# Twenty transposes of the identity at the start, one sigmoid for all gates, one projection block moved ahead of the retention

## The chip, the cores and the metric

The kernel runs on one core of one Trainium2 chip. The metric is the device time of one execution in microseconds; less is better. All data are float32; the products run in pairs of rounded parts (see below).

## What is computed

Two transformer-like blocks are applied to x (1024 tokens of 1024 channels). The first block has a root-mean-square norm, one wide input projection `h @ w_in`, a retention branch, a sparse attention branch (NSA) whose three parts are weighted by sigmoid gates, a merge of the two branches by two more gates, and a gated convolution MLP. The second block has a condition-dependent norm, an RWKV and a state-space mixer, and a second MLP. The change lies in the first block alone:

```python
h = rmsnorm(x, norm_mix)
proj = h @ w_in
(rq, rk, rv, rg, nq, kcr, vcr, ksl, vsl, kwn, vwn, ngate, ga, gb) = split(proj)
y_a = retention(rq, rk, rv, rg, ret_gn_g) @ w_ret_o          # 4 heads, chunks of 128 tokens
y_b = nsa(nq, ..., ngate, ...) @ w_nsa_o                     # gt = sigmoid(ngate): 24 gates per token
merged = sigmoid(ga) * y_a + sigmoid(gb) * y_b
x = x + merged @ w_out
...
# retention, per head: inner product within a chunk, and a state R carried from chunk to chunk
o = (q k^T * dmask) v + (q * xi) R ;  R = decay * R + (k * zeta)^T v
out = silu(g) * groupnorm(o)
```

## The kernel before

Activations lie with channels on the partitions (`a`, eight tiles of 128 x 1024, each as a rounded part `hh` and a rest `hl`). A weight block of 128 columns is loaded by `wload` (L197) into one of two `wraw` buffers, rounded by ScalarE into `whi` (L199), and its rest is made by GpSimd into `wlo` (L202, four instructions); `wload2` (L212 to L216) does the same for a block of 256 columns into `w2hi` and `w2lo` of a pool of its own. `mm3` (L226) then makes 24 matmuls of 512 columns for each half of the tokens, and `mm3t` (L234) 24 for each tile of 128 tokens. `proj` takes its result banks from the pool `PM`, which has two; a bank is free again when its result has been copied out.

The order is made by a planner: each engine has its own list of instructions, in the order in which a simulated timeline found them ready, with the order of the program as priority. On the chip each engine, and each of the queues that issue DMAs (all of this kernel's on SP), works through its list strictly in order.

The stretches that the change touches, in the order of time:

- `first_norm` (L854 on) loads x in eight tiles. For each, ScalarE sums the squares (L867), DVE scales (L281, L869), and after four tiles TensorE turns them by `transpose` (L179), a product with the identity `ident`. ScalarE and DVE copy the result out as `hh` (L877) and `hl` (L878). The identity and the ones come by the first two DMAs.
- `values_gates` (L421 on) projects values and the 24 gates of each token: eight tiles, three times eight matmuls each (L234). The bank is read by ScalarE (L452, the copy L439, the sigmoid L440) and DVE (L453). `compress` (L456 on), which stands behind it in the program, uses a Gelu (L474).
- The attention follows, with 23 projection blocks (`gate_out`, L663 on, whose results go to `d_gab`) woven into it. 28 such blocks exist; the five left over are the function `rest`.
- `retention` runs four heads and then calls `rest()`. A head (`retention_head`, L671 on) projects its values with `wload2` and `mm3t`, then works through eight chunks that hang on one another by the state R, and writes `d_yr` (L748). Its pools lie in the memory that the attention gives back. Beside the heads a side job reads `w_ada` on DVE.
- `merge` loads `d_yr` back as `yrh`, `yrl` (L777, L778), makes the sixteen halves `w_nsa_o` x `yn`, each multiplied with a gate that is loaded from `d_gab` (L343), put through the sigmoid L784 and used in L802, and then the `w_ret_o` x `yr` halves. The gates have three buffers.

Of the kernel before, what the change touches and what calls it, by code (L numbers as in the profile page):

```python
# [9 lines left out]
F32 = mybir.dt.float32  # L10
F32R = mybir.dt.float32r
AF = mybir.ActivationFunctionType
# [72 lines left out]
    return c  # L85


LINE = 512
FIRST = 16512
TOP = 480  # L90
# [28 lines left out]
class Ctx:  # L119
# [26 lines left out]
    def fill(self, pool, at=0):  # L146

        n = -(at + pool.current_size() // 128) % LINE
        if n:
# [128 lines left out]
    def rsqrt(self, r, x, scale, eps):  # L278
# [3 lines left out]
        nc.scalar.activation(r, r, AF.Sqrt)  # L282
        nc.vector.reciprocal(r, r)

    def products(self):

        ins = self.nc.cur_bb.bb.instructions
        out = [i for i in ins[self.n_ins:] if i.engine == mybir.EngineType.PE]
        self.n_ins = len(ins)
        return out  # L290
# [102 lines left out]
class Nsa:  # L393
# [27 lines left out]
    def values_gates(self, tp):  # L421

        g, nc, w_in = self.g, self.g.nc, self.w_in
        w = [tp.tile([128, KT, 280], F32R, name=f"vw{x}") for x in "hl"]
        for c0, c, n in ((0, C_VS, 128), (128, C_VW, 128), (256, C_NG, 24)):
            raw = g.W.tile([128, KT, 128], F32, name="wraw", bufs=2)[:, :, :n]
            nc.sync.dma_start(raw, w_in[:, c:c + n].rearrange("(k p) n -> p k n", p=128))
            hi, lo = (z[:, :, c0:c0 + n] for z in w)
            nc.scalar.activation(hi, raw, AF.Copy)
            nc.gpsimd.tensor_sub(lo, raw, hi.bitcast(F32))  # L430
        self.new_values()
        for i in range(8):
            ps = g.PM.tile([128, 512], F32, name="mm")
            g.mm3t(ps[:, :280], w, self.a, slice(i * 128, (i + 1) * 128))
            v = ps[:, :256].rearrange("p (b g c) -> p b g c", b=2, g=2)
            self.split_values(self.vst[i // 4][:, i % 4], v[:, :, 0])
            if i % 4 == 0:
                v1 = g.st.tile([128, 512], F32, name="st").rearrange("p (i b c) -> p i b c", i=4, b=2)
            nc.scalar.copy(v1[:, i % 4], v[:, :, 1])  # L439
            nc.scalar.activation(self.gate[:, i], ps[:, 256:280], AF.Sigmoid)  # L440
            if i % 4 == 3:
                nc.sync.dma_start(self.v1(i // 4), v1.rearrange("p i b c -> p i (b c)"))

    def v1(self, t):
        return self.dv[t * 512:(t + 1) * 512].rearrange("(i p) c -> p i c", p=128)
# [216 lines left out]
def gate_out(g, a, w_in, c, dst, n):  # L662

    def ev(t, ps):
        o = g.st.tile([128, 512], F32, name="st")
        g.evac(t, o, ps)
        g.nc.sync.dma_start(dst[n * 128:(n + 1) * 128, t * 512:(t + 1) * 512], o)
    g.proj(w_in[:, c:c + 128], a, ev)
# [82 lines left out]
def retention(g, a, w_in, gn_g, D_, yp, side_job, rest, early):  # L751


    with ExitStack() as cx:
        P = {n: cx.enter_context(g.pool("r" + n)) for n in ("vp", "tp")}
        P.update({n: cx.enter_context(g.pool("r" + n, b, space=PSUM)) for n, b in (("p1", 2), ("p2", 2), ("p3", 1))})
        sp = cx.enter_context(g.pool("rsj"))
        P.update({n: g.const(n, P["tp"]) for n in ("zeta", "xi")})
        for h in range(4):
            retention_head(g, a, w_in, gn_g, D_["gab"], D_["yr"], h, P, early)  # L760
            if h == 0:
                yn = load_split(g, yp, D_["yn"], 4, "yn")
            if h == 1:
                r = side_job(sp)
        rest()
    return r, yn


def load_split(g, pool, src, nk, name):

    out = tuple([pool.tile([128, S], F32R, name=f"{name}{x}{k}") for k in range(nk)] for x in "hl")
    for t in range(2):
        get = g.stream(src, t, g.st)
        for k in range(nk):
            x = get(k)
            sl = slice(t * 512, (t + 1) * 512)
            g.nc.scalar.activation(out[0][k][:, sl], x, AF.Copy)  # L777
            g.nc.vector.tensor_sub(out[1][k][:, sl], x, out[0][k][:, sl].bitcast(F32))  # L778
    return out
# [64 lines left out]
def params1(g, I):  # L844
    par = g.params("a", [("norm_mix", col(I["norm_mix"][0])), ("norm_ffn", col(I["norm_ffn"][0])), ("norm_final", col(I["norm_final"])),
                         ("gn_g", col(I["ret_gn_g"][0])), ("b1_k", col(I["cmp_b1_k"][0])), ("b1_v", col(I["cmp_b1_v"][0])),
                         ("pos_k", I["cmp_pos_k"][0].rearrange("(l r) d -> l (r d)", r=2)),
                         ("pos_v", I["cmp_pos_v"][0].rearrange("(l r) d -> l (r d)", r=2))])
    par.update(g.params("b", [("conv_w", I["conv_w"][0].rearrange("i (r p) -> (i r) p", p=128)), ("conv_b", col(I["conv_b"][0]))]))
    return par  # L850


def first_norm(g, gain, a):

    nc = g.nc
    with g.pool("xl", 8) as lp, g.pool("xs", 2) as tp, g.pool("xlp", 4, space=PSUM) as pp:
        tiles = []
        for i in range(8):
            x = lp.tile([128, D], F32, name="xin")
            nc.sync.dma_start(x, g.I["x"][0][i * 128:(i + 1) * 128, :])  # L860
            tiles.append(x)
            if i == 3:
                gain = gain()
        for i, x in enumerate(tiles):
            ss = g.small((128, 1))
            sq = tp.tile([128, D], F32, name="xsq")
            nc.scalar.activation(sq, x, AF.Square, accum_out=ss)  # L867
            g.rsqrt(ss, ss, 1.0 / D, EPS)
            nc.vector.tensor_scalar(x, x, ss, None, op0=OP.mult)  # L869
            if i % 4 == 3:  # L870
                sl = slice((i - 3) * 128, (i + 1) * 128)
                for k in range(KT):
                    ps = pp.tile([128, 512], F32, name="xtp")
                    for j in range(4):
                        g.transpose(ps[:, j * 128:(j + 1) * 128], tiles[i - 3 + j][:, k * 128:(k + 1) * 128])
                    hi, lo = a[0][k][:, sl], a[1][k][:, sl]
                    nc.scalar.activation(hi, ps, AF.Copy, scale=gain[:, k:k + 1])  # L877
                    nc.vector.scalar_tensor_tensor(lo, ps, gain[:, k:k + 1], hi.bitcast(F32), op0=OP.mult, op1=OP.subtract)  # L878
# [3 lines left out]
CUT = (12, 11)  # L882
# [44 lines left out]
def nsa_phase(g, par, D_):  # L927


    I = g.I  # L930
    w_in, gab = I["w_in"][0], D_["gab"]
    hp = g.alloc("hp", side="right")
    a = tuple([hp.tile([128, S], F32R, name=f"h{x}{k}") for k in range(KT)] for x in "hl")
    g.st = g.alloc("st", 3)
    g.W = g.alloc("W")

    def gain():
        par.update(params1(g, I))
        return par["norm_mix"]
    first_norm(g, gain, a)  # L940
    cols = [C_RG + 128 * n for n in range(8)] + [C_GA + 128 * n for n in range(16)]
    fill = [(24 + 2 * h + e, c + 128 * h) for h in range(EARLY) for e, c in enumerate((C_RQ, C_RK))]
    fill += [(n, cols[n]) for n in [*range(8), *range(16, 24), *range(8, 16)]]
    with ExitStack() as cx:
        N = Nsa(g, a, w_in, par, D_["yn"], D_["nv"], cx)
        with g.pool("cp") as cp:
            N.cmp_proj(cp)
            N.group_proj(0)
            N.values_gates(cp)
            N.compress(cp)  # L950
        N.tp = cx.enter_context(g.pool("at", 2))
        for n, b in (("pct", 1), ("pth", 2), ("ptl", 2)):
            N.tp.tile([128, 512], F32R, name=n, bufs=b)
        for gr in range(2):
            if gr:
                N.group_proj(gr)
            N.select(gr)
            parts = N.attend(gr)
            for n, c in fill[gr * CUT[0]:CUT[0] + gr * CUT[1]]:
                gate_out(g, a, w_in, c, gab, n)  # L960
            beside_attention(g.tc, parts, g.products())
    return a, hp, lambda: [gate_out(g, a, w_in, c, gab, n) for n, c in fill[sum(CUT):]]


def block1(g, par, D_, side_job):

    I = g.I
    a, hp, rest = nsa_phase(g, par, D_)
    with g.pool("mgy") as yp:
        r, yn = retention(g, a, I["w_in"][0], par["gn_g"], D_, yp, side_job, rest, EARLY)  # L970
        hp.release()
        m = merge(g, D_, I, yn)
    g.WX = g.alloc("WX")
    return r, m
# [1048 lines left out]
```

## Time and profile before

| | us |
|---|---|
| median of 3 runs | 3440.11 |
| lowest and highest of the 3 | 3436.26, 3441.54 |
| the profiled execution, its time | 3434.05 |
| the profiled execution, first to last instruction (span) | 3432.3 |
| TensorE busy in the span | 3325.8 |

The profiled execution lies 6.06 us under the median of the runs, and 1.75 us of its own time lie outside its span. "PE" is TensorE, "DVE" VectorE, "ACT" ScalarE, "POOL" GpSimd, "SP" the queue that issues the DMAs. L with a number is a line of the kernel; a transpose has the helper's line L179 wherever it is called from. The mean granted TensorE clock of the span is 0.989 of full speed.

### The profile page before, as it was taken

What the parts mean: (1) busy time and instruction counts of PE and PEld (TensorE: products, weight loads), DVE (VectorE), ACT (ScalarE), POOL (GpSimd) and SP (SyncE); (2) the same over time, 40 slices, a digit from 0 to 9 for tenths busy, and PEclk for the clock granted to TensorE, in tenths of its full rate; (3) what the DMA queues carried; (4) which work ended last, traced back from release to release, by engine and by line L of the source; (5) the groups of instructions that cost most, each with busy time, mean ns of one, the idle gap of its engine ahead of it and who ended that gap; (6) DMA issues with size and microseconds to landing.
All of it is one profiled execution on the core that took longest, in us unless ns stands there. A gap on an engine that the chain in (4) does not pass through costs nothing. (4 is left out here: it accounts for less than half of the span.)

```text
span 3432.3 us, 51013 instructions
## 1 busy us (share of the span) xinstructions
PE 3325.8 (97%) x19080; PEld 2702.8 (79%) x19080; DVE 1593.4 (46%) x3313; ACT 1323.1 (39%) x2165; POOL 1699.6 (50%) x2221
## 2 busy tenths in 40 slices
PE   8999999999999999999999999999999999999998
PEld 6888888898788777888887777778777777688887
DVE  4356556555523674355564454653634343341112
ACT  5245446422334322344244344433443343342223
POOL 2343444321245656576776454355764343365554
PEclk9999999999999999999999999899999999999999
DMA  4211221455634434344533222144442122263332
GB/s 150 67 60 46 64 66 42 142 165 189 212 114 142 126 103 144 92 120 146 188 107 115 67 62 70 56 157 129 138 134 70 48 68 65 90 194 98 89 95 93
DMA packets 519826, 371.13 MB, mean 108 GB/s; under 512 B 31724, under 2 KB 455834, under 8 KB 518810
## 3 DMA queue, kind: packets, MB, share of 16 engines
q1 hardware_dynamic: 519578, 367.86, 34.8%
q8 instruction: 151, 2.47, 0.3%
q14 instruction: 97, 0.79, 0.1%
HBM read 313.44 MB, written 54.03 MB: 107 GB/s over the span
## 5 line engine op out<-in xcount | busy, mean ns | idle before, releaser
L202 POOL TENSOR_TENSOR wlo<-wraw,whi 128x256 fp32r<-128x256 f32 (+1 forms) x1552 | 1196.4, 801 | 1081.8 <-ACT whi L199 570.2
L199 ACT ACTIVATE whi<-wraw 128x1024 fp32r<-128x1024 f32 (+2 forms) x460 | 417.2, 909 | 792.6 <-PE mm L226 454.0
L226 PE MATMUL mm<-fh,whi 128*128 128x512 f32 x976 | 399.5, 411 | 3.2 <-ACT whi L199 2.5
L226 PE MATMUL mm<-fl,whi 128*128 128x512 f32 x976 | 390.4, 401 | 8.0 <-DVE fl L337 8.0
L226 PE MATMUL mm<-fh,wlo 128*128 128x512 f32 x976 | 269.3, 405 | 0.0
L226 PE MATMUL mm<-hh,whi 128*128 128x512 f32 x640 | 258.5, 404 | 3.7 <-DVE kc L255 2.8
L226 PE MATMUL mm<-hl,whi 128*128 128x512 f32 x640 | 259.0, 405 | 0.0
L226 PEld LDWEIGHTS mm<-fl,whi 128*128 128x128 f32 x976 | 184.9, 190 | 48.6 <-DVE fl L337 11.2
L226 PEld LDWEIGHTS mm<-fh,whi 128*128 128x128 f32 x976 | 184.7, 190 | 47.5 <-issue 4.7
L226 PE MATMUL b<-fh,whi 128*128 128x512 f32 x544 | 212.3, 390 | 0.4 <-DVE yo L255 0.4
L226 PE MATMUL b<-fl,whi 128*128 128x512 f32 x544 | 211.9, 390 | 0.0
L226 PEld LDWEIGHTS mm<-fh,wlo 128*128 128x128 f32 x976 | 179.2, 190 | 40.1 <-issue 3.3
L226 PE MATMUL mm<-ah,whi 128*128 128x512 f32 x429 | 177.0, 415 | 11.0 <-ACT ah L1621 8.4
L226 PE MATMUL mm<-hh,wlo 128*128 128x512 f32 x640 | 178.3, 400 | 0.0
L226 PE MATMUL mm<-al,whi 128*128 128x512 f32 x429 | 172.5, 403 | 0.2 <-DVE al L1622 0.2
L226 PE MATMUL b<-fh,wlo 128*128 128x512 f32 x544 | 139.1, 392 | 5.2 <-POOL wlo L202 5.2
L226 PEld LDWEIGHTS mm<-hh,whi 128*128 128x128 f32 x640 | 121.2, 189 | 25.8 <-issue 3.2
L226 PEld LDWEIGHTS mm<-hl,whi 128*128 128x128 f32 x640 | 121.2, 189 | 20.8
L226 PEld LDWEIGHTS mm<-hh,wlo 128*128 128x128 f32 x640 | 117.0, 188 | 21.8
L597 POOL TENSOR_SCALAR s<-s,ast 128x640 f32<-128x640 f32 (+7 forms) x128 | 88.1, 708 | 78.4 <-DVE ast L595 48.9
L226 PE MATMUL mm<-ah,wlo 128*128 128x512 f32 x429 | 126.0, 405 | 0.2 <-POOL wlo L202 0.2
L226 PEld LDWEIGHTS b<-fh,wlo 128*128 128x128 f32 x544 | 101.6, 188 | 29.1 <-POOL wlo L202 8.6
(600 smaller groups left out, 6976.8 us busy)
## 6 DMA issues: line engine op xcount, KB each, us to landing
wraw<-in_w_up SPq DMA_DIRECT2D x88, 512.0 KB
wraw<-in_w_in SPq DMA_DIRECT2D x84, 512.0 KB
ada_w<-in_w_ada SPq DMA_DIRECT2D x96, 256.0 KB
wraw<-in_ffn_w_gate SPq DMA_DIRECT2D x44, 512.0 KB
wraw<-in_ffn_w_up SPq DMA_DIRECT2D x44, 512.0 KB
wraw<-in_w_out SPq DMA_DIRECT2D x32, 512.0 KB
d_gab<-st SPq DMA_DIRECT2D x56, 256.0 KB
wraw<-in_w_down SPq DMA_DIRECT2D x48, 256.0 KB
```

Of the source, the lines that this page charges most:

```text
L199: nc.scalar.activation(hi[:, :kt], raw[:, :kt], AF.Copy)
L202: nc.gpsimd.tensor_sub(lo[:, sl], raw[:, sl], hi[:, sl].bitcast(F32))
L226: self.nc.tensor.matmul(ps, w[x][:, k], a[y][k][:, t * 512:(t + 1) * 512], start=i == 0, stop=i == 3 * kt - 1)
L597: nc.gpsimd.tensor_scalar(sb[r][:, :n], sb[r][:, :n], st[:, 2, r:r + 1], 1.0, op0=OP.mult, op1=OP.mult)
```

## The change

Three edits are made. `warm` is new: after the first four loads of x are issued, TensorE turns the identity twenty times into one bank, and DVE copies the last result over the identity itself, so that each later transpose depends on it. In `values_gates` the sigmoid of each of the eight tiles becomes a copy, and one sigmoid over all eight stands behind the loop. `rest` becomes a list of five functions; the first is called ahead of the four heads, the other four where all five were.

```diff
+WARM = 20
@@ class Ctx
+    def warm(self):
+        ps = self.PN.tile([128, 512], F32, name="pn")
+        for i in range(WARM):
+            self.transpose(ps[:, i % 4 * 128:(i % 4 + 1) * 128], self.ident)
+        self.nc.vector.tensor_copy(self.ident, ps[:, (WARM - 1) % 4 * 128:((WARM - 1) % 4 + 1) * 128])
@@ def values_gates
-            nc.scalar.activation(self.gate[:, i], ps[:, 256:280], AF.Sigmoid)
+            nc.scalar.copy(self.gate[:, i], ps[:, 256:280])
             if i % 4 == 3:
                 nc.sync.dma_start(self.v1(i // 4), v1.rearrange("p i b c -> p i (b c)"))
+        nc.scalar.activation(self.gate, self.gate, AF.Sigmoid)
@@ def retention
+        rest[0]()
         for h in range(4):
             retention_head(g, a, w_in, gn_g, D_["gab"], D_["yr"], h, P, early)
...
-        rest()
+        for x in rest[1:]:
+            x()
@@ def first_norm
             if i == 3:
+                g.warm()
                 gain = gain()
@@ def nsa_phase
-    return a, hp, lambda: [gate_out(g, a, w_in, c, gab, n) for n, c in fill[sum(CUT):]]
+    return a, hp, [lambda n=n, c=c: gate_out(g, a, w_in, c, gab, n) for n, c in fill[sum(CUT):]]
```

## Rows read from the trace of the kernel before

**Rows 1.** The page: busy us of each engine (share of the span), instructions.

```profile
PE 3325.8 (97%) x19080; PEld 2702.8 (79%) x19080; DVE 1593.4 (46%) x3313; ACT 1323.1 (39%) x2165; POOL 1699.6 (50%) x2221
```

**Rows 2.** The waits of TensorE: who waited for whom, us in all, times, longest.

```profile
PE mm L234 <- ACT w2hi L214: 3.3, 2, 2.3
PE mm L234 <- ACT gate L440: 3.1, 1, 3.1
...
PE mm L226 <- DVE kc L255: 2.8, 1, 2.8
...
PE mm L226 <- DVE yb L802: 2.5, 3, 1.5
```

**Rows 3.** The timeline, start: start us, us, engine, line, operation, count, [idle before <-releaser].

```profile
6.60 0.15 DVE L281 TENSOR_SCALAR sm<-sm 128x1 f32<-128x1 f32 x1 [6.60 <-ACT xsq L867]
...
9.12 1.12 PE L179 MATMUL xtp<-c_ident,xin 128*128 128x128 f32 x4 [9.12 <-DVE xin L869]
...
13.58 1.06 ACT L867 ACTIVATE xsq<-xin 128x1024 f32<-128x1024 f32 x1 [1.11 <-DMA xin<-in_x]
...
17.61 2.82 PE L179 MATMUL xtp<-c_ident,xin 128*128 128x128 f32 x12 [2.99 <-DVE hl L878]
...
22.34 0.48 PE L226 MATMUL mm<-hh,whi 128*128 128x512 f32 x1
...
29.71 0.60 PE L179 MATMUL xtp<-c_ident,xin 128*128 128x128 f32 x4
```

**Rows 4.** Windows: stretch, length, busy us of PE, PEld, DVE, ACT, POOL (instructions), PEclk, DMA, GB/s.

```profile
17.60:21.60 4.00, 3.82 (x17) 3.31 (x17) 3.47 (x9) 4.00 (x9) 0.00 (x0) 1.00 1.12 353
...
107.80:111.20 3.40, 3.38 (x16) 3.38 (x17) 0.29 (x1) 0.49 (x3) 0.00 (x0) 0.58 0.68 214
...
638.20:643.60 5.40, 5.40 (x33) 5.40 (x33) 2.38 (x2) 0.96 (x2) 5.40 (x7) 0.68 0.74 237
...
1583.80:1587.00 3.20, 0.12 (x2) 0.04 (x1) 2.32 (x3) 0.69 (x2) 2.97 (x4) 1.00 0.00 0
1587.00:1600.00 13.00, 13.00 (x91) 12.25 (x92) 3.78 (x8) 3.42 (x7) 4.78 (x6) 1.00 0.46 150
```

**Rows 5.** The timeline around the gates of the third to eighth tile of tokens.

```profile
106.01 0.27 ACT L439 COPY st<-mm 128x128 f32<-128x128 f32 x1 [2.58 <-DVE vst L453]
106.28 1.28 ACT L440 ACT_TABLE_LOAD   x1
107.58 0.19 ACT L440 ACTIVATE gate<-mm 128x24 f32<-128x24 f32 x1
...
107.82 2.23 PE L234 MATMUL mm<-vwh,hh 128*128 128x280 f32 x8 [3.08 <-ACT gate L440]
...
126.15 1.28 ACT L474 ACT_TABLE_LOAD   x1 [2.62 <-PE oacc L473]
```

**Rows 6.** The timelines of ACT, POOL and PE at the retention's start.

```profile
636.12 2.00 ACT L214 ACTIVATE w2hi<-wraw 128x1024 fp32r<-128x1024 f32 x2
...
637.26 6.46 POOL L216 TENSOR_TENSOR w2lo<-wraw,w2hi 128x256 fp32r<-128x256 f32 x8 [4.41 <-ACT w2hi L214]
...
638.17 1.21 PE L234 MATMUL mm<-w2hi,hh 128*128 128x256 f32 x8 [2.34 <-ACT w2hi L214]
```

**Rows 7.** The last block (windows, L226), the timeline of ACT, and tiles of the merge.

```profile
894.85:905.87 11.02, 10.98 (x49) 9.13 (x50) 1.00 0.65 213
...
842.57 1.67 ACT L784 ACTIVATE st<-st 128x512 f32<-128x512 f32 x3
...
L778 DVE TENSOR_TENSOR yrl<-st,yrh x16: 684/693/1124, 906.8 to 935.3; 128x512 fp32r<-128x512 f32 x16
L802 DVE TENSOR_TENSOR yb<-mm,st x16: 683/692/692, 908.8 to 953.4; 128x512 f32<-128x512 f32 x16
L343 SPq DMA_DIRECT2D st<-d_gab x16: 319/320/531, 909.6 to 954.1; - x16
...
L226 PE MATMUL mm<-yrh,whi x86: 389/389/389, 953.1 to 1009.8; 128*128 128x512 f32 x86
```

## The prediction
> **What bounds the kernel now.** I read the page first, and in it the share of TensorE: 3325.8 of 3432.3 us are busy [rows 1]. So the end moves only by what shortens TensorE's list: its waits, 106.5 us in all, and the stretches in which it runs at the lower of its two clocks. The second view is therefore the list of TensorE's waits, which says what ended each [rows 2]; the reader is to see that none of them is large, and that two carry names that the change touches: `w2hi` (3.3 us in two waits, the longest 2.3) and `gate` (one of 3.1). Third come the windows, for the granted clock around these waits [rows 4], and last the timelines of the three places [rows 3, 5, 6] and of the merge, from which a block is taken [rows 7]. The work of TensorE itself is the same before and after, but for the twenty transposes.
>
> **The twenty transposes.** The first real transposes start at 9.12, after DVE's scaling [rows 3]. Twelve transposes at 17.61 take 2.82 us, 0.235 each, where later four take 0.60, 0.15 each, so the chip is at 1.2 GHz there and at 2.4 GHz later [rows 3]. Twenty at 0.235 are 4.7 us. They need only the identity, which stands ahead of x in the DMA queue; x's first tile is in by 5.5, since its sum reaches DVE at 6.60 and costs ScalarE 1.06 us [rows 3]. So I put the twenty between about 3 and 8, with DVE's copy behind them, in the idle 9.12 us: cost zero. If the identity came as late as x, they would end at 5.5 + 4.7 = 10.2, 1.1 us after 9.12. And if the planner puts DVE's copy ahead of the scaling at 6.60, DVE's list stands until the copy is done, 1.4 us with an end at 8, 3.6 us with one at 10.2; who waits for that are the first four tiles. What hides it is ScalarE's wait of 1.11 us for the fifth tile of x at 13.58 [rows 3]; uncovered is 0.3 to 2.5 us.
>
> The gain lies between nothing and what a raised clock could take from the transposes behind: 3.82 busy us at 17.6 to 21.6 [rows 4], half of them 1.9. I take nothing, because in that stretch ScalarE is busy for 4.00 of 4.00 us, and because between 9.12 and 17.61 TensorE has long waits, so a clock raised at 8 would have to outlive these. The first matmul at 22.34 needs ScalarE's results and not only TensorE's. Term: 0, ends -1.9 and +2.5.
>
> That transposes raise the clock at all is shown here: only transposes run ahead of 22.34 [rows 3, 4], and the same operation is faster soon after. The Trainium skill says the opposite (TensorE: Matmul & The Clock Gate, Part 4): a transpose does not count as activity, so the full clock does not engage. By that page the twenty could do nothing; by the rows they could raise the clock, which keeps a rival alive below.
>
> **The gates.** At 106.28 ScalarE loads a table for 1.28 us, and only then reads the gates at 107.58 and frees the bank; TensorE, which has two banks here, has waited 3.08 us for it [rows 5]. The load stands behind the copy L439 and ahead of the sigmoid [rows 5], so a copy runs on the table that is in, and the bank comes free 1.28 us earlier. The eight copies cost what the eight sigmoids cost. What is late next is DVE's list, which lets ScalarE start only at 106.01 [rows 5]; 3.08 - 1.28 = 1.80 us stay. The late sigmoid costs ScalarE one load and some 0.3 us (128 x 192, between the 0.19 us for 24 columns [rows 5] and the 1.06 for 1024 [rows 3]) after the last tile. It is hidden by ScalarE's idle 2.62 us ahead of 126.15 [rows 5], where the Gelu's load stands already; without that cover it would delay the Gelu by 1.6 us, beside which TensorE has other work. The attention reads the gates later still.
>
> After the wait the granted clock over 3.40 us is 0.58, a loss of 0.42 x 3.40 = 1.43 us [rows 4]. Whether it falls after 1.80 us of idling is open: after the 2.34 us at 635.83 it does fall, 0.68 over 5.40 us [rows 4, 6], after more than 3 us ahead of 1587 it doesn't, 1.00 [rows 4]. I take half. Term: -1.28 - 0.71 = -1.99, ends -1.28 and -2.71.
>
> The Trainium skill (ScalarE: Activation LUTs, What ACT_TABLE_LOAD costs) adds a drain of about 1.38 us to each load. Worked out from that page, as an estimate, the sum below would be 1.38 us lower. The rows disagree: the load ends at 107.56 and the sigmoid starts at 107.58 [rows 5].
>
> **The block ahead of the retention.** The first head starts with `w2hi`, whose memory the attention has just given back, so ScalarE can begin only at 636.12, and TensorE idles 2.34 us until 638.17 [rows 6]. Then comes the lower clock: 0.32 x 5.40 = 1.73 us lost [rows 4]. A projection block is 11.0 us of matmuls [rows 7] and uses the `wload` buffers, which exist already; `w2hi` needs 2.0 us of ScalarE and `w2lo` 6.46 of GpSimd [rows 6], both shorter than 11.0. So wait and low clock go: -2.34 - 1.73 = -4.07. It moves with its DMAs: one `wraw` load ahead of the two of `wload2`, and two writes to `d_gab`. With two `wraw` buffers the second load of `wload2` now stands on SP until GpSimd has made the block's `wlo`; behind it on SP stand the attention's last writes. I count that as hidden. At worst the wait stays as it is: ends -4.07 and 0.
>
> At the back 11.0 us of cover go. The last block ran at 894.85 to 905.87, beside the end of the chain of head four [rows 7]. `w_ret_o` starts at 953.1, and its last operand is made at 935.3 + 0.7 = 936.0 [rows 7]: 17.1 us to spare. The block takes 11.0 of them, 6.1 stay. Term: 0. Bounds: below, the two longer waits on `yb` (2.5 us [rows 2]) may go too; above, the whole block, 11.0, may be lost (the rival on the gates' loads).
>
> **Sum.** 0 - 1.99 - 4.07 + 0 = -6.06 us. Against the profiled execution that is 3434.05 - 6.06 = 3428.0; against the median of the runs, which lies 6.06 above that execution, 3440.11 - 6.06 = 3434.05. I forecast the median: 3434.1.
>
> **Rivals.** (1) The block is drawn into the attention's end. The planner may start its matmuls as soon as its weights are there, since they are held to nothing; then TensorE meets `w2hi` as before, and only the gates count: 3440.11 - 1.99 = 3438.1. For it: the weights can be ready well ahead of 636. Against: the 23 blocks woven in leave TensorE full there. This is the change not doing what it says.
>
> (2) Slower: the merge keeps its pace. Its halves on `w_nsa_o` need sixteen gates; three are made early, at 842.57, and the others are loaded only from 909.6 on, behind the `d_yr` loads on SP [rows 7]. If these loads stay tied to the end of the chain while the matmuls come 11.0 us earlier, TensorE uses up three gates and two banks and waits, and the hole at the front reappears at the back: +11.0, so 3440.11 - 6.06 + 11.0 = 3445.1. It decides at 6.06 us of the 11.0. For it: two waits on `yb` stand there already [rows 2]. Against: a gate's buffer comes free when `yb` is made, at 908.8 + 0.7, and the load follows at 909.6, at once [rows 7]; so the loads follow TensorE rather than the chain.
>
> (3) The raised clock lasts, and the first norm gains its 1.9 us: 3432.2. Against: ScalarE is full there.
>
> (4) The planner's order changes elsewhere. Every list is made from simulated times, and the change moves these from the first microsecond on. The wait on `kc` (2.8 us [rows 2]) shows what one such order costs, and it can vanish or be repeated: 3434.1 - 2.8 = 3431.3, or 3436.9.
>
> **How the numbers follow.** Forecast 0.47 (its own range 3430.5 to 3437.5: the terms' ends and the runs' spread), rival 1 0.14, rival 2 0.13, rival 3 0.06, rival 4 0.20, half on each side. 0.2%, about what a measurement of this kernel can tell from no change, is 6.9 us: faster means under 3433.2, slower above 3447.0. The forecast is 0.9 us from the first bound, so nearly half of it counts as faster, with most of rival 3 and the lower half of 4: 0.39. Rival 2 crosses the upper bound only with the spread, and the unforeseen is there: 0.10. The rest, 0.51, is no change that can be told. The range 3425 to 3445 takes in the lower cases with the terms at their better ends and half of rival 2.
>
> **What would show it.** Right: no row of `gate` among TensorE's waits and no table load between the tiles of L234; matmuls of L226 ahead of the first L234 of head one, no wait on `w2hi` of 2 us, and the clock at 1.00 there; `w_ret_o` following `w_nsa_o` without a wait. Wrong: first transposes after 9.12, an idle TensorE in the merge of more than the 2.5 us of `yb`, the first L234 of the retention waiting for `w2hi` as before, or new waits in the second block, which the change doesn't touch.

## The result, and the profile after

The change makes the kernel slower: 3462.17 us median of 5 runs (3453.98 to 3470.4) against 3439.78 (3430.78 to 3441.54, 5 runs) on the same chip, a ratio of 1.0078 with a 95% interval of 1.0062 to 1.0095. The forecast was 3434.1 with 3425 to 3445: the sign is wrong, and the time lies 17 us above the range. The profiled execution after took 3460.71 us with a span of 3458.9, so 26.6 us more span than before, at a granted clock of 0.985 in place of 0.989.

The page after, in the columns of [rows 1]:

```profile
PE 3342.6 (97%) x19100; PEld 2708.2 (78%) x19100; DVE 1590.3 (46%) x3314; ACT 1321.6 (38%) x2165; POOL 1696.0 (49%) x2221
```

The share of TensorE hardly tells anything: 97% in both. What tells is a cut of the span at points that both kernels have: the first selection product of the attention, the first L234 of the heads, the first product on `yn`, the first on `yr` and the last on `yr` with `whi`. The windows between these, first of before, then of after (columns as in [rows 4]):

```profile
168.20:638.20 470.00, 464.23 (x2435) 384.74 (x2433) 282.78 (x809) 240.29 (x492) 193.18 (x272) 1.00 0.18 55
638.20:905.90 267.70, 262.14 (x1634) 235.79 (x1635) 145.25 (x303) 76.16 (x124) 57.49 (x69) 0.99 0.59 188
905.90:953.10 47.20, 44.63 (x193) 35.61 (x192) 22.58 (x32) 24.67 (x39) 13.32 (x18) 1.00 0.67 217
953.10:1037.90 84.80, 84.80 (x376) 70.20 (x375) 22.07 (x31) 24.82 (x38) 44.55 (x47) 1.00 0.34 106
```

```profile
167.40:649.00 481.60, 476.59 (x2482) 393.86 (x2481) 283.16 (x809) 241.83 (x493) 199.84 (x282) 1.00 0.18 55
649.00:921.80 272.80, 258.34 (x1587) 228.74 (x1586) 142.67 (x301) 73.76 (x121) 49.12 (x60) 0.97 0.56 178
921.80:973.50 51.70, 46.49 (x193) 36.81 (x192) 23.30 (x34) 27.00 (x42) 12.84 (x18) 0.97 0.69 218
973.50:1058.30 84.80, 84.80 (x375) 70.22 (x374) 22.37 (x31) 24.83 (x38) 44.47 (x47) 1.00 0.34 106
```

By stage, worked out from these rows:

| stage | before, us | after, us | difference |
|---|---|---|---|
| start to the first selection product | 168.2 | 167.4 | -0.8 |
| attention; after: with the block's 48 matmuls | 470.0 | 481.6 | +11.6 |
| the heads, from the first L234 to the first product on `yn` | 267.7 | 272.8 | +5.1 |
| `w_nsa_o` x `yn` | 47.2 | 51.7 | +4.5 |
| `w_ret_o` x `yr` | 84.8 | 84.8 | 0.0 |
| the rest of the program | 2394.4 | 2400.6 | +6.2 |
| span | 3432.3 | 3458.9 | +26.6 |

The third line is the answer in short. The block left this stage, so it should have become 11.0 us shorter [rows 7]; it became 5.1 us longer. TensorE stands idle in it for 272.80 - 258.34 = 14.5 us, before for 267.70 - 262.14 = 5.6, and the lower clock is granted for some 13.5 us, before only for the stretch of [rows 4] at its start. Two windows of after, with the clock at 0.50:

```profile
733.20:743.40 10.20, 8.83 (x31) 7.04 (x30) 3.50 (x7) 1.21 (x2) 2.40 (x3) 0.50 0.71 222
828.80:832.10 3.30, 3.30 (x14) 2.94 (x13) 1.51 (x3) 0.50 (x2) 0.00 (x0) 0.50 0.98 294
```

The waits of TensorE after, from the retention to the merge (columns as in [rows 2]), are no longer the ones of before: `w2hi` is smaller, and new ones on `sg`, `ada_a` and `st` stand there.

```profile
PE r L180 <- DVE sg L757: 4.7, 3, 2.6
PE mm L227 <- DVE yb L814: 4.0, 3, 2.5
PE pn L1970 <- DVE ada_a L1965: 1.9, 3, 0.9
PE mm L235 <- ACT w2hi L215: 1.7, 1, 1.7
PE mm L227 <- DVE st L256: 1.6, 2, 0.9
```

The last line of the table, 6.2 us in code that no edit touches, is not of the change alone. TensorE is busy 2.5 us longer in it and idle 3.7 us longer (2323.97 of 2400.60 us, before 2321.48 of 2394.40, for 13612 matmuls each). In the traces of the runs below that carry one or both of the edits that cost nothing, a point of the second block (its first product on `mh`, 1592.8 in before) lay 11 to 17 us later too, so the profiled execution of before is a short one. I explain the 20.4 us up to the end of `w_ret_o`, and leave the 6.2 open.

### The profile page after: what moved, and what is told of

It is laid out like the page before. It is cut to its first block, busy times and chain, and to the rows that moved or that the text cites. A ratio compares the mean times of both kernels' runs of the same rounds, so it can differ in the third digit from the quotient of the medians.

```text
span 3458.9 us, 51048 instructions
## 1 busy us (share of the span) xinstructions
PE 3342.6 (97%) x19100; PEld 2708.2 (78%) x19100; DVE 1590.3 (46%) x3314; ACT 1321.6 (38%) x2165; POOL 1696.0 (49%) x2221
## 5 line engine op out<-in xcount | busy, mean ns | idle before, releaser
L602 ACT ACTIVATE s<-s,amn 128x640 f32<-128x640 f32 (+7 forms) x128 | 93.9, 734 | 81.2 <-DVE amn L598 76.4
```

The lines of the kernel that those rows point to most:

```text
L602: nc.scalar.activation(sb[r][:, :n], sb[r][:, :n], AF.Exp, bias=init, scale=-1.0, accum_out=st[:, 0, r:r + 1])
```

## The experiments

Each run is compared with runs of the kernel before beside it on the same chip; the ratio carries the comparison. Letters for theories are those of the expectations.

**One edit at a time.** Runs e1 to e3 make one of the three edits alone, e4 the first two together (the diffs are those of the section on the change).

> The twenty transposes alone. Theory A (the block moved ahead of the retention costs it all, by the new order of the retention's lists): no change that can be told, 0.998 to 1.002 of the kernel before; the first product stands at +0 to +2 us in the trace and everything behind it keeps that distance. Rival B (the twenty transposes shift the start, and the shift runs through the planner's timeline into the retention): 1.004 or more, with the retention's rows at +10 us and over.

> The one sigmoid alone. Theory A: 0.9985 to 1.000 of the kernel before, -1.3 to -2.7 us in the trace at the first scores, by the step of the prediction, and the same distance to the end but for stretches of the lower clock. Rival C (the late sigmoid delays something behind it): 1.002 or more.

> The block ahead of the retention alone. Theory A: 1.005 to 1.008 of the kernel before (+17 to +27 us); in the trace the first product of the retention's values stands at about +11, the last projection block at +16 to +19, the first product of w_ret_o at +20 or more. Rival B: 0.997 to 1.002. If half of the loss is that of the runs' lower clock in the second block and not of the block, 1.002 to 1.004.

> The twenty transposes and the one sigmoid, without the block moved: is what the two bring additive, and is it a version that beats both kernels? Theory A: 0.998 to 1.001 of the kernel before, 20 us and more under the changed kernel. Rival B: 1.004 or more.

| run | edits | median, us (runs) | ratio, 95% interval |
|---|---|---|---|
| e1 | twenty transposes | 3438.54 (12) | 1.0001, 0.9983 to 1.0019 |
| e2 | one sigmoid | 3437.59 (12) | 0.9994, 0.9979 to 1.0010 |
| e3 | block ahead | 3459.84 (6) | 1.0062, 1.0041 to 1.0084 |
| e4 | transposes and sigmoid | 3437.18 (12) | 0.9997, 0.9979 to 1.0014 |

The block ahead costs it all: 0.62% of 3440 are 21 us. The other two edits are not to be told from nothing. The traces say the same where only the first block is counted. From the first selection product to the first product on `yr` the executions with the block in its old place take 784.9 (before), 789.7 (e1), 791.3 (e2) and 788.3 us (e4), those with the block ahead 806.1 (after), 810.7 (e3) and 810.4 (e15). A stage of one execution is thus known to some 6 us: the heads that take 267.7 us in before take 271.1, 273.7 and 270.7 in e1, e2 and e4. The change itself, run once more beside later experiments (e15), gave 1.0061 (1.0040 to 1.0081), 3461.63.

> The whole change once more, beside the others on one chip, as their base: 3456 to 3466 by every theory.

**The staging buffers.** In e3 the first long wait behind the block is ScalarE's. Its timeline (columns as in [rows 3]) shows the roundings of `yn` waiting for their loads, and head two's `w2hi` behind them; TensorE's next L234 waits 4.34 us for that:

```profile
664.10 0.63 ACT L779 ACTIVATE ynh<-st 128x512 fp32r<-128x512 f32 x1 [6.01 <-DMA st<-d_yn]
...
674.39 1.88 ACT L779 ACTIVATE ynh<-st 128x512 fp32r<-128x512 f32 x3 [6.48 <-DMA st<-d_yn]
676.18 0.35 ACT L255 COPY rv<-mm 128x256 f32<-128x256 f32 x1
676.43 2.00 ACT L214 ACTIVATE w2hi<-wraw 128x1024 fp32r<-128x1024 f32 x2
...
678.49 1.86 PE L234 MATMUL mm<-w2hi,hh 128*128 128x256 f32 x7 [4.34 <-ACT w2hi L214]
```

The loads of `yn` are late since the block's two results take two of the three `st` buffers: the loads are issued from 649.0 on, in before from 633.4 on. So theory S: give the block other buffers, and the time returns.

```diff
-    def ev(t, ps):
-        o = g.st.tile([128, 512], F32, name="st")
+    def ev(t, ps):
+        o = buf() if buf else g.st.tile([128, 512], F32, name="st")
...
-        rest[0]()
+        rest[0](lambda: P["tp"].tile([128, 512], F32, name="sg", bufs=2))
```

> The block ahead of the heads as before, but its two results go through the two buffers `sg` that head one doesn't need before its end, and no longer through the three `st` buffers. Theory S (the staging buffers: the block's results hold `st` ahead of the loads of yn, ScalarE's list has the roundings of yn ahead of head two's w2hi, and TensorE waits behind it): the loads of yn are issued near 634 again, ScalarE has no wait of 6 us for them, head two's first L234 doesn't wait, and the some 20 us that the block ahead costs go for the larger part: 3437 to 3450. Theory O (the planner's other order in the heads, whatever the buffers): 3455 to 3463. Theory B (the cover that is gone at the back): 3455 to 3463, with the waits of the merge as they are with the block ahead alone.

Measured: 3459.29, ratio 1.0078 (1.0061 to 1.0094). ScalarE's waits for the loads of `yn` went from 13.6 us in all to 1.2, and no wait of 0.8 us or more on `w2hi` stands in the heads; nothing of the time came back. Two waits further on took the place of the one removed (timeline of TensorE in e5):

```profile
736.38 0.66 PE L179 MATMUL r<-c_ident,rk 128*128 128x128 f32 x4 [3.12 <-DVE sg L747]
...
756.61 0.38 PE L1959 MATMUL pn<-c_ones,ada_a 128*128 128x1 f32 x2 [4.17 <-DVE ada_a L1954]
```

Theory S falls, though its wait was real and its cure did what it should: the longest wait of a trace was not the cause.

**Another place, and another time for the side job.** In e6 the block stands behind head one and the loads of `yn`; in e7 it is ahead as in the change, and the side job `ada` (96 loads of 256 KB, and 96 operations of DVE) is called after head three.

```diff
# e6
-        rest[0]()
...
+                rest[0]()        # behind yn, at h == 0
# e7
-            if h == 1:
+            if h == 2:
                 r = side_job(sp)
```

> The block stands behind head one and behind the loads of yn, and the back still has one block less. Theory S: `st` goes to yn first, so the time returns to that of before with the wait of 2.3 us on w2hi: 3437 to 3446. Theory B (one block less beside the end of head four's chain and of cover for the merge): the place in front doesn't matter, 3455 to 3463. Theory O: any block among the heads changes the order of the heads; 3450 to 3463.

> The block ahead as in the change, and the side job (`ada`, 96 loads on SP) is called after head three instead of after head two. Theory S: the wait of 4.3 us at 674 with the low clock behind it stays, and what is lost later (the loads of sg that stand on SP behind those of the side job) may go: 3447 to 3458. Theory Q (the queue: sg's loads behind the side job's are the whole loss): 3437 to 3444. Theories O and B: 3455 to 3463.

Measured: e6 3456.61, ratio 1.0069 (1.0052 to 1.0085); e7 3442.66, ratio 1.0031 (1.0005 to 1.0057). The place of the block doesn't matter much, which is against S once more. The side job does: e7 gives back most. In before 25 of its loads are issued between the last output transpose of head one and that of head two, in after 28, in e7 two (ten stand beside head one, the others later). Theory B, by which the cover at the back is what lacks, is against e7, where the back has one block less as well.

**Is it the block, or the block beside the side job?** e8 and e9 cut the side job to an eighth (the second block then gets other shifts and gains), without and with the block ahead. e10 calls the whole side job ahead of head one. e11 is the control for e7.

```diff
# e8 (from before), e9 (block ahead)
-        for k in range(KT):
+        for k in range(1):
             raw = tp.tile([128, 512], F32, name="ada_w", bufs=2)
# e10 (block ahead)
         rest[0]()
+        r = side_job(sp)
         for h in range(4):
...
-            if h == 1:
-                r = side_job(sp)
# e11 (from before)
-            if h == 1:
+            if h == 2:
                 r = side_job(sp)
```

> The kernel before, its side job cut to the first of each eight loads (12 of 96 loads and 12 of 96 DVE operations stay; the second block's shifts and gains are then other numbers). Theory D (pace: from head two on, the side job's stream through two buffers, one load after the other, sets the pace of the lists): TensorE is as busy beside the whole stream as it can be in before (some 183 of 187 us), so little is won: 3430 to 3440. Theory O (order) says nothing of this run. It is the base for the next.

> The block ahead, and the side job cut to an eighth in the same way. Theory D: without the stream nothing holds the heads to a pace, so the block's 11 us in front come back at the end of the retention: within 5 us of the run with the eighth and no block moved, so about 3430 to 3442. Theory B (the cover that is gone beside the end of head four's chain and in the merge): 12 us or more above that run, 3446 to 3460. Theory O (any order of the heads with the block ahead is worse): 10 us or more above it as well.

> The block ahead, and the whole side job called behind it and ahead of head one, not after head two. Theory D: the stream starts some 20 us sooner than with the block ahead alone (first operation near 655 in place of 679) and ends near 890 to 895 in place of 915, so most of the 20 us comes back: 3436 to 3447. Theory O or B: 3453 to 3465.

> The kernel before with the side job after head three, the control for the run that had the block ahead too (3442.7). Theory D: the heads are bound by TensorE in before, so the later side job wins nothing by itself: 3436 to 3446, and the block ahead then costs within 5 us. Theory O or B: the late side job is a gain by itself, 3422 to 3432, and the block ahead costs 12 to 20 us on top of it.

| run | block ahead | side job | median, us (runs) | ratio, 95% interval |
|---|---|---|---|---|
| e8 | no | an eighth | 3434.94 (10) | 0.9967, 0.9949 to 0.9984 |
| e9 | yes | an eighth | 3433.49 (10) | 0.9987, 0.9965 to 1.0008 |
| e11 | no | after head three | 3444.09 (10) | 1.0012, 0.9996 to 1.0027 |
| e7 | yes | after head three | 3442.66 (7) | 1.0031, 1.0005 to 1.0057 |
| e10 | yes | ahead of head one | 3452.28 (10) | 1.0044, 1.0026 to 1.0061 |

With an eighth of the side job the block ahead costs between -1.5 us (medians) and 7 (0.0020 of 3440, by the ratios), with the late side job between -1.4 and 6.5; with the whole stream in its place, 19 to 21. Each of these four ratios is known to 5 to 9 us only. The traces, over the same stretch as above, give 5.5 us with the eighth (777.1, then 782.6) and -4.9 with the late side job (791.9, then 787.0). So most of the loss is not the block's, nor the back's, nor that of any other order of the heads: it is there where the block is ahead and the stream runs beside head two. The windows show it, here the heads of e8, then of e9:

```profile
637.10:896.00 258.90, 258.82 (x1634) 235.95 (x1635) 83.16 (x219) 76.21 (x124) 49.86 (x69) 0.99 0.34 108
```

```profile
651.70:897.40 245.70, 244.91 (x1575) 223.94 (x1574) 80.39 (x216) 72.50 (x119) 41.09 (x58) 1.00 0.33 102
```

In this stage the prediction's arithmetic comes out: TensorE idles 0.1 and 0.8 us, and the heads get 13.2 us shorter, where a block of 11.0 and the low clock's 1.73 make 12.7. (The wait on `w2hi` lies ahead of the stage.)

Theory D in its strict form, that the stream's own length is the bound, falls by e10. The stream does what D says there (DVE's first operation of it starts at 663.9 in place of 679.1, its last at 889.6 in place of 914.5), and only 7.6 us of the median come back, where 13 and more were expected. Called ahead of head one, the stream still has 28 loads between the last output transposes of head one and head two, as many as in after, and there head two falls another 6.7 us behind.

**By which list?** The stream meets the heads on SP and on DVE. e12 issues its loads by GpSimd, on a queue of its own; e13 is the control without the block ahead. e14 leaves the stream on SP and issues only the sixteen loads of `sg` by ScalarE; e16 is its control.

```diff
# e12 (block ahead), e13 (from before)
-            nc.sync.dma_start(raw, w[k * 128:(k + 1) * 128, m * 512:(m + 1) * 512])
+            nc.gpsimd.dma_start(raw, w[k * 128:(k + 1) * 128, m * 512:(m + 1) * 512])
# e14 (block ahead), e16 (from before)
-            nc.sync.dma_start(sg, gab[n * 128:(n + 1) * 128, sl])
+            nc.scalar.dma_start(sg, gab[n * 128:(n + 1) * 128, sl])
```

> The block ahead, and the 96 loads of the side job issued by GpSimd on a queue of its own in place of SP. Theory Q (SP's list: the loads of sg, the writes of d_yr and the weights stand between loads of the side job that wait for a buffer): most of the 20 us goes, 3436 to 3446, and the sg loads of head two are no longer the last thing that ScalarE waits for. Theory V (DVE's list: the side job's operations stand in it and wait for their loads, and the heads' operations stand behind them, whatever queue the loads come by): 3452 to 3464.

> The kernel before with the side job's loads on GpSimd's queue, the control. Theory Q: SP is not what binds there, 3434 to 3442. Theory V: the same, 3434 to 3446. If it is as slow as the block ahead, GpSimd's list suffers from the waiting issues (w2lo and wlo behind them), and the run above can't be read.

> The block ahead, and only the sixteen loads of sg issued by ScalarE on a queue of its own; the side job's loads stay on SP. Theory Q: sg no longer stands behind the side job, about half of the 20 us goes: 3440 to 3452. Theory V: 3454 to 3464.

> The kernel before with the sixteen loads of sg issued by ScalarE on a queue of its own, the control for the block ahead with the same queue (3451.0). Theory Q: in before the loads of sg lose little on SP (6.7 us of ScalarE's time in head two, beside which TensorE has other work), so 3434 to 3444, and the block ahead costs 8 to 15 us on top of it. If it is slower than 3446, the other queue costs something by itself, and the other run understates what sg's place on SP costs.

| run | block ahead | queue | median, us (runs) | ratio, 95% interval |
|---|---|---|---|---|
| e13 | no | stream by GpSimd | 3456.95 (4) | 1.0047, 1.0032 to 1.0062 |
| e12 | yes | stream by GpSimd | 3447.12 (10) | 1.0022, 1.0005 to 1.0040 |
| e16 | no | `sg` by ScalarE | 3441.03 (10) | 1.0012, 0.9996 to 1.0029 |
| e14 | yes | `sg` by ScalarE | 3450.97 (10) | 1.0035, 1.0020 to 1.0051 |

With `sg` on another queue the block ahead costs 8 (ratios) to 10 us (medians) in place of 19 to 21, as theory Q says, and the control shows that the queue alone brings before nothing. With the stream off SP the block ahead is a gain, of 9 to 10 us against its control. But that control is itself 16 to 17 us slower than before: GpSimd's list waits 96.5 us for DVE to give the stream's buffers back, and TensorE has a wait of 6.0 us in the merge. By what was written ahead of e13, e12 can then not be read. It would not part SP's list from DVE's (theory V) in any case, since the order on DVE differs too: in e12 the first two L747 (the product that writes `sg`) stand ahead of the stream's operations, at 712.12 and 713.50, in after (L757) they don't. So what is shown is that the place of `sg` on SP is worth about half.

What happens is to be read in head two. The side job stands in the trace of before as (tile `ada_w`):

```profile
L1950 SPq DMA_DIRECT2D ada_w<-in_w_ada x96: 327/328/941, 657.8 to 886.5; - x96
```

Here is SP in after, from the end of head one on (timeline, DMA issues), then DVE in after, then DVE in before:

```profile
717.91 0.57 SPq L758 DMA_DIRECT2D d_yr<-sg  x1
719.34 1.99 SPq L1963 DMA_DIRECT2D ada_w<-in_w_ada  x2
721.44 0.38 SPq L198 DMA_DIRECT2D wraw<-in_w_in  x1
721.86 0.58 SPq L758 DMA_DIRECT2D d_yr<-sg  x1
723.04 0.50 SPq L752 DMA_DIRECT2D sg<-d_gab  x1
724.54 1.12 SPq L1963 DMA_DIRECT2D ada_w<-in_w_ada  x2
728.33 0.33 SPq L752 DMA_DIRECT2D sg<-d_gab  x1
```

```profile
715.31 0.56 DVE L1967 TENSOR_SCALAR ada_a<-ada_w,ada_c 128x512 f32<-128x512 f32 x1
715.91 1.11 DVE L1965 SCALAR_TENSOR_TENSOR ada_a<-ada_w,ada_c,ada_a 128x512 f32<-128x512 f32 x1
716.94 0.74 DVE L757 SCALAR_TENSOR_TENSOR sg<-r,pc_a,sg 128x512 f32<-128x512 f32 x1
718.57 0.75 DVE L1965 SCALAR_TENSOR_TENSOR ada_a<-ada_w,ada_c,ada_a 128x512 f32<-128x512 f32 x1 [0.89 <-DMA ada_w<-in_w_ada]
720.23 0.75 DVE L1965 SCALAR_TENSOR_TENSOR ada_a<-ada_w,ada_c,ada_a 128x512 f32<-128x512 f32 x1 [0.91 <-DMA ada_w<-in_w_ada]
720.90 0.75 DVE L757 SCALAR_TENSOR_TENSOR sg<-r,pc_a,sg 128x512 f32<-128x512 f32 x1
```

```profile
699.85 0.75 DVE L747 SCALAR_TENSOR_TENSOR sg<-r,pc_a,sg 128x512 f32<-128x512 f32 x1 [1.48 <-PE r L179]
...
701.02 0.75 DVE L1954 TENSOR_SCALAR ada_a<-ada_w,ada_c 128x512 f32<-128x512 f32 x1
701.69 0.74 DVE L747 SCALAR_TENSOR_TENSOR sg<-r,pc_a,sg 128x512 f32<-128x512 f32 x1
```

Two lists hold each other. A load of `sg` needs its buffer, which the write of `d_yr` gives back. The write follows L757 on DVE at once (717.68 to 717.91, and 721.65 to 721.86). But L757 stands behind operations of the stream on DVE, which wait for loads of `ada_w` on SP, and these loads need buffers that the operations give back. The order in each list is the planner's: in before the first L747 is ahead of the stream's operations, in after two of them are ahead of L757. So the first two L757 come 4.9 and 8.9 us after head one's first output transpose (712.0), where in before the first two L747 come 1.4 and 3.2 us after it (698.5). The next two loads of `sg` stand behind the writes and, on SP, behind more of the stream. They are issued at 723.04 and 728.33, 11.0 and 16.3 us after that transpose; in before at 703.03 and 706.11, 4.5 and 7.6 us after it. Until `sg` has come, ScalarE stands, and with it DVE, which holds the two banks that head two's transposes need. The timelines show it at ScalarE's table load for `sg`, with the idle time ahead of it: first after, with the transposes that wait behind, then e12:

```profile
729.02 1.28 ACT L753 ACT_TABLE_LOAD   x1 [9.81 <-DMA sg<-d_gab]
...
731.79 0.66 PE L180 MATMUL r<-c_ident,rk 128*128 128x128 f32 x4 [2.59 <-DVE sg L757]
```

```profile
717.93 1.28 ACT L743 ACT_TABLE_LOAD   x1 [4.24 <-DMA sg<-d_gab]
```

In e12 it starts 7.1 us after head one's first output transpose (710.8), in before 8.9 (707.42), in after 17.0. And the delay against before of head one's and head two's last output transposes is 15.8 and 30.5 us in after, 18.4 and 32.0 in e3, 14.5 and 20.7 in e14, 12.2 and 12.4 in e12, 12.2 and 12.2 in e9: where SP has nothing of the stream (e12) or an eighth (e9), head two adds nothing to what head one was late. How the loss that e14 leaves divides between SP's list and DVE's no run shows.

The lengths of the two stages in all these runs, each from the same two points as above (first line: before and e3):

| stream | heads without / with the block ahead, us | `w_nsa_o` x `yn` without / with |
|---|---|---|
| on SP, beside head two | 267.7 / 277.4 | 47.2 / 51.5 |
| an eighth | 258.9 / 245.7 | 48.2 / 52.4 |
| after head three | 271.1 / 252.8 | 50.8 / 50.8 |
| on GpSimd's queue | 276.3 / 255.5 | 58.4 / 53.6 |
| on SP, `sg` on ScalarE's queue | 272.4 / 265.0 | 47.4 / 53.2 |

**Both cures on the whole change.** e17 is the change with `sg` on ScalarE's queue and the side job after head three.

> The whole change, with the loads of sg on ScalarE's queue and the side job after head three: the two cures that each gave something back, together. Theory Q: the heads go as with an eighth of the side job up to its start, 3432 to 3444. If the cures only move the wait, 3445 to 3455.

Measured: 3442.72, ratio 1.0007 (0.9990 to 1.0024). The 0.8% are gone, and no gain over before is to be seen. No kernel that computes the whole beats before by more than the noise.

## Why the prediction was wrong, step by step

**The twenty transposes: right.** They run from 2.62 to 6.71, where 3 to 8 was said; the first real ones start at 9.27 in place of 9.12, and DVE's scaling at 6.55 is not held. Term 0, and e1 shows none. The clock rose within the burst and fell again with the first real transposes. The granted clock of the profile can't show the rise, since it says 1.00 over 0 to 5 us of before too, where TensorE does nothing; the durations can. The transposes of the burst take 421 ns (median), the last ones 273, the first three real ones 309 to 413, and most later ones 421 again (after: tile `pn` from 2 us on, the same from 6.25 on, and windows):

```profile
L180 PE MATMUL pn<-c_ident x20: 272/421/475, 2.6 to 6.4; 128*128 128x128 f32 x20
...
L180 PE MATMUL pn<-c_ident x5: 272/273/404, 5.9 to 6.4; 128*128 128x128 f32 x5
...
9.60:22.00 12.40, 8.16 (x33) 5.71 (x31) 8.41 (x24) 10.23 (x24) 0.00 (x0) 0.50 0.97 326
```

So rival 3 doesn't hold, for one of the reasons given: the waits between. The rule of the Trainium skill that was weighed there (TensorE: Matmul & The Clock Gate, Part 4) would have the clock stay down; the second of these rows is against it.

**The gates: right, and not to be measured.** No table load stands between the tiles any more, and the wait is 1.66 us, where 3.08 - 1.28 = 1.80 was said [rows 5]. The granted clock over 106 to 112 is 1.00, so the stretch of [rows 4] is gone as well: the better end of the term. At the first selection product -0.8 us is left of it, and that shows nothing: in the runs with neither of these two edits the point lies anywhere from 166.8 to 171.8.

```profile
107.88 0.27 ACT L448 COPY st<-mm 128x128 f32<-128x128 f32 x1 [3.94 <-DVE vst L463]
108.04 0.18 ACT L449 COPY gate<-mm 128x24 f32<-128x24 f32 x1
...
108.28 1.31 PE L235 MATMUL mm<-vwh,hh 128*128 128x280 f32 x8 [1.66 <-ACT gate L449]
```

The wait is 1.42 us shorter. By the drain that the Trainium skill adds to each load (ScalarE: Activation LUTs, What ACT_TABLE_LOAD costs) it would have been 1.28 + 1.38 = 2.66, as an estimate; the trace doesn't show that.

**The front: the cover right, the time not won.** The wait on `w2hi` ahead of the first head is gone, and so is the low clock behind it: the block's last matmuls end where L235 starts.

```profile
643.46 0.50 PE L227 MATMUL mm<-hh,whi 128*128 128x512 f32 x1 [0.78 <-DVE st L256]
...
647.22 1.98 PE L227 MATMUL mm<-hh,wlo 128*128 128x512 f32 x8
649.03 1.12 PE L235 MATMUL mm<-w2hi,hh 128*128 128x256 f32 x8
```

Rival 1 came in half: 23 of the block's 48 matmuls were drawn into the attention's end, and the 25 left were enough to cover `w2hi`. But the stage up to the first L235 grew by 11.6 us, where 11.0 - 2.34 = 8.7 was due. TensorE idles in it 5.0 us in place of 5.8, so other waits took the place of this one (0.51, 0.23 and 0.78 us from 641 on), and it is busy 12.4 us longer for a block of 11.0. This repeats: the stage takes 481.6 to 484.4 us in all ten traces with the block ahead of head one, and 469.9 to 470.1 in all others.

**Between the front and the back: wrong, and this is the step that failed.** The sum put the block's 11.0 us at the front and took 11.0 us off at the end of head four, "17.1 us to spare", term 0. I read the two ends and took the 210 us between them as work that only slides: for the heads the sum has no term. The end did nearly what was said. From head four's last output transpose to the first product on `yn` it is 11.0 us in before and 1.7 in after. Here are that end and head two (from the end of head one's last output transpose to that of head two's), first of before, then of after:

```profile
706.60:760.70 54.10, 54.10 (x353) 49.60 (x352) 34.41 (x77) 14.43 (x24) 6.74 (x8) 1.00 0.62 196
...
895.20:905.90 10.70, 10.70 (x49) 8.85 (x48) 1.41 (x2) 3.66 (x5) 0.62 (x1) 1.00 0.64 211
```

```profile
722.40:791.10 68.70, 63.28 (x381) 56.01 (x379) 36.93 (x80) 16.02 (x26) 11.42 (x14) 0.93 0.55 173
...
920.40:921.80 1.40, 1.40 (x8) 1.13 (x7) 0.00 (x0) 0.28 (x1) 0.00 (x0) 1.00 0.77 243
```

What lies between did not slide. After is 10.8 us late at the first L235, 15.8 at the last output transpose of head one, 30.5 at head two's (28 more matmuls stand in it, TensorE idles 5.4 us, and the clock is 0.93) and still 25.2 at head four's. So the heads became 5.1 us longer in place of 11.0 + 1.73 = 12.7 shorter. That is 17.8 of the 32.7 us between the sum (-6.06) and the span (+26.6); the merge is 4.5, the front 2.9, the start 1.2, and the rest of the program 6.2. What was left out stood in the trace of before: 96 loads of the side job, in the same in-order list as the heads' own loads and writes. The prediction names SP, but only for the block's weights ("I count that as hidden") and the gates' loads of the merge.

**Rival 2: four tenths of its price.** The merge does keep its pace: 4.5 us longer, with the waits on `yb` at 4.0 in place of 2.5 us and a stretch of low clock (0.50 from 945 to 948). Not the gates alone do it: in this stage of after ScalarE waits 12.7 us for the loads of `d_yr` and 8.5 for those of the gates. With an eighth of the side job the merge gets longer too (48.2 to 52.4 us), so there this part is the block's own. Together with the front it is why e9, without the collision, gains nothing: its trace reaches the first L234 14.5 us later than e8's, counted from the first selection product, where 8.7 was due; the heads are 13.2 shorter, and the merge is 4.2 longer. No run tries a cure for either.

**Rival 4: the right kind, mis-sized.** "The planner's order changes elsewhere" was priced by one wait, 2.8 us [rows 2]. What came was a shift of one head against a stream that shares two strict lists with it, with 8.9 us more of idle time in waits of at most 2.6 us each, and half of 10 us more at the lower clock. The chance of 0.10 for slower was taken from rival 2's edge and the unforeseen.

**What stays open.** How the loss divides between SP's list and DVE's, and whether another order of the same instructions would avoid it; why the block ahead makes the attention's end 3 us longer than its matmuls and its cover account for; how the second block's 6.2 us come about; and why the stream on GpSimd's queue is slow without the block and less so with it.

## What to carry to other kernels

A block moved from the back of a stage to its front shifts everything between against whatever runs by its own clock; before calling it free at both ends, look for such a stream (a side job's loads, a prefetch) that shares in-order lists with the chain, a queue of loads and writes or an engine's, and price the shift by the turnaround of a buffer there, not by one wait. The longest wait in the trace after may be a mere symptom: removing it moved the loss to the next one (e5). A pair of runs with the suspected stream cut down, without and with the edit, told cause from symptom in one step.

## What the runs showed of the hardware

In a burst of twenty transposes of the identity, 4.09 us long, the clock rises although no other product has run: most of them take 421 ns, the last ones 273. It is at 0.50 again from 9.60 on, with TensorE busy for 8.16 of 12.40 us.

An issue of a 256 KB load took 0.54 us of GpSimd's list (e12, median) against 0.33 on SP, but the wait for the buffer stands ahead of it in the same list and cost far more: 96.5 us of GpSimd's time in e13.
